# Start, Hyena filters, softmax ends and the last group of a two-block transformer on one core: loads reordered, groups of four, a lag of one chunk

## The chip, the core and the metric

The kernel runs on one core of a Trainium2 chip. Five engines work side by side, each on its own list of instructions: TensorE (PE: matmuls and transposes; its weight loads are shown as PEld), VectorE (DVE), ScalarE (ACT), GpSimd (POOL) and SyncE (SP), which issues most of the transfers (DMA). They wait for each other by semaphores. Data lie in SBUF, matmuls write to PSUM, and inputs, outputs and some intermediate results lie in HBM. The metric is the device time of one execution in microseconds (us), the median of the runs shown.

## What is computed

Two transformer blocks follow one another on x (512 tokens of 1024 channels) with a context of 256 tokens. The first is one layer: retention and mLSTM heads run in both directions after having run over the context, then a SwiGLU feed-forward. The second has four layers with the mixers latent attention (MLA), sliding-window attention (SWA), Hyena, and latent attention again.

```python
# first block, one layer
mod = silu(c) @ w_ada + b_ada                    # six vectors: sh1, sc1, g1, sh2, sc2, g2; the same for ctx
hc = rms_norm(ctx, norm1_gain) * (1 + csc1) + csh1
feats_c = mixer_inputs(hc, w_in, ...)            # keys, values, gates of the context: start states
hx = rms_norm(x, norm1_gain) * (1 + sc1) + sh1
feats_x = mixer_inputs(hx, w_in, ..., rope)      # query, key, value, gate; rope on the retention heads
x = x + g1 * mixer_output(scans(feats_x, states))
x = rms_norm(x + g2 * swiglu(...), final_gain)
# second block
for layer in range(4):
    hx = rmsnorm(x, g_pre[layer]) * (1 + scale_x) + shift_x; hc = ... of ctx
    yx, yc = (mla_mixer, swa_mixer, hyena_mixer, mla_mixer)[layer](hx, hc, ...)
    x = x + gate_x * rmsnorm(yx, g_post[layer])
    ctx = ctx + gate_c * rmsnorm(yc, g_post[layer])      # not in the last layer
# swa: softmax over [context scores, band scores, one sink column]; hyena: two long convolutions with
# filters made by a small sine network from 64 hidden channels, on x and on ctx
```

## The kernel before

Activations lie channel-major: eight tiles of 128 channels by 512 tokens (x) or 256 tokens (context). Almost every matmul is made in three passes of a split operand: a value is cut into a high and a low part (`split`, L396: ACT casts at L397, DVE subtracts at L398), and `mac` (L436) issues high by high, high by low, low by high (L441, L442, L443). Weights come as 512 KB loads into four buffers (`wload`, L400, tile `raw`) and are split into `whi` and `wlo`. Tiles named `b` (128 by 512) have 53 buffers, `t` ten, `P` eight.

The order of the work is written out with generators: `weave` (L192) takes steps of several generators in proportion to the numbers beside them, and `islice` takes only the first steps of one. `self.mods(n)` takes n steps of the stream of modulation vectors (`mod_stream`, L520): each vector takes four steps, each step two loads of 512 KB and 16 matmuls with 32 columns of weights (L504). `need(i)` draws from the stream until vector i is there.

**Start** (`first_block`, L603). SP issues the row vectors (`rows`), the filter network's constants (`filter_setup`, L1776), x, ctx, and then the `w_ada` loads of the first vectors. `load_T` (L476) transposes x and ctx on TensorE, `Rms` (L222) sums squares, and its root is taken by one small matmul (L242), DVE (L244) and POOL (L245), and spread by `over_columns` (L1373). `norm1` (L639) applies norm and modulation to x (L570 and L576 on DVE, L575 on ACT), stores x to HBM (`xd`, L645), and then does the same for the context. `ahead` holds the first key weights. `dense` (L798) makes, for a pair of heads, keys, context keys, values, context values, start states, and then for each head a query and a gate.

**Hyena filters.** `filters` runs beside the feed-forward layer. In `filter_unit` (L1855) each tile takes one matmul with 128 rows of weights (L1873) and one with 64 rows (L1874), which adds the low part.

**Softmax** (`softmax`, L1376) is called once for each head and block of 128 queries: maximum (L1380), its negative times the scale (L1382; with a sink L1384), exponential with its sum (L1385), for a sink one more exponential (L1387) and an add (L1388), and the reciprocal (L1389). `stageA` of MLA and SWA calls it; `stageB` transposes P and multiplies by V. In SWA's `stageB` the low part of P is multiplied by 64 columns of V (L1738, L1741).

**Hyena** (`hyena`, L1907). `conv(i, c)` (L1953) is the two long convolutions of chunk c (256 channels) of x (i = 0, 20 steps) or of the context (i = 1, 14 steps). Chunk c runs beside the projections of chunk c + 1; the last chunk runs beside eight steps of modulation vectors and the preloads of the output projection.

**End** (`layer_end`, L1244). `product(z)` (L1264) multiplies a group of 256 tokens by the output weights, copies to SBUF (L1277) and sums squares; `rest(z)` (L1284) takes the root, scales, adds x from HBM (L1308, L1309) and, in the last layer, `store` (L1333) transposes to token-major (L1340), copies (L1341) and stores (L1342). The `rest` of the last group is left over for the very end.

## Time and profile before

| what | us |
|---|---|
| median of 3 runs | 2915.62 (2914.16 to 2920.24) |
| the profiled execution | 2918.76 |
| its span on the core | 2917.0 |
| TensorE busy | 2787.1 |
| VectorE busy | 1814.9 |
| ScalarE busy | 1334.4 |

The profile is one execution. The kernel is one long list of work for TensorE, in stages that use the other engines to different degrees; TensorE's idle time lies at the two ends and in the attention and Hyena stages. A matmul's shown duration includes the time in which it overlaps its neighbours, so what a matmul costs is read from the distance between the starts of two that follow one another.

### The profile page before, as it was taken

How to read it: one execution, taken by the hardware profiler on the slowest of the kernel's cores; microseconds unless marked ns; L12 is line 12 of the kernel's file. 1: busy time of each engine (PE TensorE's matmuls, PEld its weight loads, DVE VectorE, ACT ScalarE, POOL GpSimd, SP SyncE). 2: the span in 40 equal slices, each digit the busy share in tenths (PEclk: the TensorE clock that was granted, in tenths of full speed). 3: DMA queues.
4: the chain of work that ended last, by engine and by line, in shares of the span. 5: the costliest groups of instructions: out<-in, count | busy, mean ns of one | idle time of the engine just before them, and what ended most of it. 6: DMA issues, size and time to landing. Idle time of an engine off the chain costs nothing. (4 is left out here: it accounts for less than half of the span.)

```text
span 2917.0 us, 44103 instructions
## 1 busy us (share of the span) xinstructions
PE 2787.1 (96%) x17106; PEld 2364.2 (81%) x17106; DVE 1814.9 (62%) x3775; ACT 1334.4 (46%) x2610; POOL 128.8 (4%) x158
## 2 busy tenths in 40 slices
PE   7999999999999999999999999989999998999998
PEld 4888878887777787888889877778888886887887
DVE  6665455555655556246768577788576777754774
ACT  4344344346455433345555566675332223544553
POOL 1000000000000000000000000000021122000000
PEclk8999999999999999999999999999999999999998
DMA  7233232544555536321234241123132226432122
GB/s 264 86 111 123 73 101 84 168 154 141 164 158 163 170 112 209 108 67 44 68 93 156 64 131 42 35 71 117 62 95 84 84 80 195 130 97 63 56 82 69
DMA packets 365830, 318.98 MB, mean 109 GB/s; under 512 B 17511, under 2 KB 326517, under 8 KB 365620
## 3 DMA queue, kind: packets, MB, share of 16 engines
q1 hardware_dynamic: 365204, 315.99, 35.2%
q8 instruction: 134, 2.20, 0.3%
q14 instruction: 76, 0.62, 0.1%
q0 software_dynamic: 416, 0.17, 0.0%
HBM read 273.90 MB, written 42.21 MB: 108 GB/s over the span
## 5 line engine op out<-in xcount | busy, mean ns | idle before, releaser
L441 PE MATMUL mm<-b,whi 128*128 128x512 f32 (+1 forms) x2548 | 895.8, 352 | 4.7 <-ACT whi L397 2.5
L443 PE MATMUL mm<-b,wlo 128*128 128x512 f32 (+1 forms) x2548 | 887.3, 348 | 1.2 <-DVE wlo L398 1.1
L442 PE MATMUL mm<-b,whi 128*128 128x512 f32 (+1 forms) x2548 | 887.6, 348 | 0.0
L441 PEld LDWEIGHTS mm<-b,whi 128*128 128x128 f32 x2548 | 486.1, 191 | 74.4 <-issue 5.8
L443 PEld LDWEIGHTS mm<-b,wlo 128*128 128x128 f32 x2548 | 486.1, 191 | 62.0 <-DVE wlo L398 2.3
L442 PEld LDWEIGHTS mm<-b,whi 128*128 128x128 f32 x2548 | 486.5, 191 | 60.2 <-issue 0.8
L398 DVE TENSOR_TENSOR wlo<-raw,whi 128x1024 fp32r<-128x1024 f32 (+3 forms) x286 | 292.0, 1023 | 239.7 <-ACT whi L397 224.1
L397 ACT CAST whi<-raw 128x1024 fp32r<-128x1024 f32 (+3 forms) x286 | 252.3, 885 | 397.1 <-PE mm L442 253.9
L443 PE MATMUL mm<-b 128*128 128x256 f32 (+1 forms) x628 | 189.4, 302 | 0.5 <-DVE b L398 0.3
L1385 ACT ACTIVATE P<-mm,sm 128x768 f32<-128x768 f32 (+3 forms) x176 | 127.9, 727 | 116.6 <-DVE sm L1382 68.4
L441 PE MATMUL mm<-b 128*128 128x256 f32 (+1 forms) x500 | 158.2, 318 | 8.4 <-ACT P L1385 4.6
L441 PE MATMUL mm<-b,P 128*128 128x256 f32 x560 | 161.8, 289 | 4.0 <-ACT b L575 2.8
L442 PE MATMUL mm<-b,P 128*128 128x256 f32 x560 | 160.4, 286 | 0.9 <-DVE b L576 0.8
L442 PE MATMUL mm<-b 128*128 128x256 f32 (+1 forms) x500 | 153.0, 307 | 0.4 <-DVE b L398 0.3
L1380 DVE TENSOR_REDUCE sm<-mm 128x1 f32<-128x768 f32 (+3 forms) x176 | 128.6, 733 | 39.7 <-PE mm L1583 23.8
L245 POOL TENSOR_TENSOR rs<-rs,mhalf 128x2 f32<-128x2 f32 (+1 forms) x44 | 42.3, 962 | 2427.2 <-DVE rs L244 2279.8
L398 DVE TENSOR_TENSOR t<-mm,t 128x512 fp32r<-128x512 f32 (+1 forms) x208 | 136.5, 663 | 15.3 <-ACT t L397 14.1
L397 ACT CAST t<-mm 128x512 fp32r<-128x512 f32 (+1 forms) x208 | 116.0, 569 | 54.8 <-PE mm L1395 51.6
L235 DVE TENSOR_TENSOR t<-t 128x256 f32<-128x256 f32 (+1 forms) x216 | 92.5, 441 | 71.9 <-ACT t L231 69.4
L1395 PE MATMUL mm<-ct,P 128*128 128x128 f32 x768 | 122.8, 276 | 13.0 <-ACT P L1385 8.2
L231 ACT ACTIVATE t<-b 128x256 f32<-128x256 f32 (+1 forms) x252 | 100.7, 431 | 67.7 <-DVE b L1101 40.9
L443 PEld LDWEIGHTS mm<-b 128*128 128x128 f32 x628 | 120.6, 192 | 5.6 <-DVE b L398 1.3
(351 smaller groups left out, 5129.7 us busy)
## 6 DMA issues: line engine op xcount, KB each, us to landing
raw<-in_w_mod_dram SPq DMA_DIRECT2D x96, 512.0 KB, 4.4
raw<-in_w_ada_dram SPq DMA_DIRECT2D x48, 512.0 KB, 3.9
raw<-in_w_in_dram SPq DMA_DIRECT2D x48, 512.0 KB, 4.0
raw<-in_w_ffn_in_dram SPq DMA_DIRECT2D x44, 512.0 KB, 4.1
raw<-in_c_w_in_dram SPq DMA_DIRECT2D x32, 512.0 KB, 4.3
raw<-in_a_w_in_dram SPq DMA_DIRECT2D x28, 512.0 KB, 4.1
ks<-t SPq DMA_DIRECT2D x48, 256.0 KB, 2.8
raw<-ks SPq DMA_DIRECT2D x24, 512.0 KB, 3.3
```

What stands on the lines that cost most here:

```text
L231: self.k.nc.scalar.activation(sq, x, AF.Square)
L235: self.k.nc.vector.tensor_tensor(self.acc, self.acc, sq, ALU.add)
L245: nc.gpsimd.tensor_tensor(s[:, 4:4 + nt], s[:, :nt], self.k.mhalf[:, :nt], ALU.pow)
L397: self.nc.scalar.copy(dst.hi, src)
L398: self.nc.vector.tensor_tensor(dst.lo, src, dst.hi.bitcast(F32), ALU.subtract)
L441: nc.tensor.matmul(ps, l.hi, r.hi, start=start and i == 0, stop=False)
L442: nc.tensor.matmul(ps, l.hi, r.lo, start=False, stop=False)
L443: nc.tensor.matmul(ps, l.lo, r.hi, start=False, stop=stop and i == n - 1)
L1380: nc.vector.tensor_reduce(s[:, 0:1], S, AX.X, ALU.max)
L1385: nc.scalar.activation(P, S, AF.Exp, bias=s[:, 1:2], scale=scale, accum_out=s[:, 2:3])
L1395: self.nc.tensor.transpose(ps[:, 128 * i:128 * i + 128], b, self.ident)
```

## The change

Five places are edited.

1. **Start.** x is issued first; the row vectors go to ACT's queue, the filter network's constants to POOL's; ctx is issued only behind the first key weights. The context's norm becomes a generator of its own (`norm1c`). The keys of the first pair are multiplied tile by tile as the norm of x gives them, in two PSUM banks; the first query and gate come ahead of the context's keys, beside `norm1c`. The stores of x to HBM come behind that. `mod_stream` gets a stop after the second vector.
2. **Hyena filters.** The low part of the filter weights gets 64 rows of zeros (a memset on POOL), and its matmul takes all 128 rows.
3. **Softmax** ends once for a group of query blocks or heads: one reciprocal of up to four columns; in SWA the four sinks share one add, one exponential and one add. SWA's low-part matmul takes all 128 columns of V.
4. **Hyena.** The context's convolution of a chunk runs a chunk later; three modulation steps move into the chunk loops, five stay at the end.
5. **End.** The last group of the last layer goes through `last`: each product is scaled by the gate on DVE and squared on ACT straight from PSUM, transposed (`turn`) to token-major in two PSUM tiles, and x is transposed beside it; behind the root four operations of 512 columns scale, add x and are stored on two queues.

```diff
@@ mod_stream
             self.have.add(i)
+            if i == 1:
+                yield
@@ first_block
-        first = self.rows(False, nc.sync)
+        inputs = [self.load_T(I["x"][0], N, X), self.load_T(I["ctx"][0], NC, C)]
+        next(inputs[0])
+        first = self.rows(False, nc.scalar)
         next(first)
-        setup = self.filter_setup()
+        self.second_setup()
+        setup = self.filter_setup(nc.gpsimd)
         next(setup)
...
-        weave((chain(inputs[0], sums(rms[0], X)), 17), (islice(units, U0), U0), self.mods(MA))
+        weave((chain(inputs[0], sums(rms[0], X)), 17), self.mods(M0 - 3))
         self.log_sigmoid(lg, lgt, 8)
-        mods = chain(self.mods(M0 - MA)[0], root(rms[0]), self.mods(8 - M0)[0])
-        weave((chain(inputs[1], sums(rms[1], C)), 17), (islice(units, U1), UW * U1), (mods, 9 - MA))
-        rms[1].root()
+        mods = chain(self.mods(3)[0], root(rms[0]), self.mods(8 - M0)[0])
+        weave((islice(units, U0), U0), (mods, 12 - M0))
         W = I["w_in"][0]
         ahead = [self.wv(W, 512)]
-        weave((norm1(), 16), (islice(units, UB), UB))
+        next(inputs[1])
@@ dense
+            if out == {(pair, ml): o}:
+                banks = [self.mm() for _ in range(2)]
+                for k, _ in enumerate(norm1()):
+                    for u in range(2):
+                        self.mac(banks[u], [(wk[k][:, 128 * u:128 * u + 128], hx[k])], k == 0, k == KT - 1)
+                    yield
...
+            if banks:
+                yield from query(0)
             kc = kv_ctx(wk)
@@ first_block
-        weave((dense(0, False), ND), (chain(idle(GD), gates()), 10 + GD), (units, UC))
+        start = dense(0, False)
+        weave((islice(start, KT), KT))
+        cf.update(tables())
+        weave((islice(start, 4), 4), (norm1c(), 28), (units, 2))
+        for k in range(KT):
+            nc.sync.dma_start(self.xd[k], X[k])
+        X.clear()
+        weave((start, ND - 4), (chain(idle(GD), gates()), 10 + GD), (units, UC))
@@ filter_head, filter_unit
-            ws.append((w, l[0:64, :]))
+            nc.gpsimd.memset(l[64:128, :].bitcast(F32), 0.0)
+            ws.append((w, l))
-                        nc.tensor.matmul(ps, x[0:64, :], l, start=False, stop=True)
+                        nc.tensor.matmul(ps, x, l, start=False, stop=True)
@@ softmax (step for each block, end for the group)
+        def step(j, S, P):
+            b = top[:, 4 + j:5 + j]
+            nc.vector.tensor_reduce(top[:, j:j + 1], S, AX.X, ALU.max)
...
+            nc.scalar.activation(P, S, AF.Exp, bias=b, scale=scale, accum_out=sums[:, j:j + 1])
+        def end(rd):
+            if sink is not None:
+                nc.vector.tensor_tensor(top[:, 0:n], sink, top[:, 4:4 + n], ALU.add)
+                nc.scalar.activation(top[:, 0:n], top[:, 0:n], AF.Exp)
+                nc.vector.tensor_tensor(sums[:, 0:n], sums[:, 0:n], top[:, 0:n], ALU.add)
+            nc.vector.reciprocal(rd[:, 0:n], sums[:, 0:n])
@@ swa stageB
+                    nc.tensor.matmul(out, v[:, g], p.hi, start=z == LS, stop=False)
+                    nc.tensor.matmul(out, v[:, g], p.lo, start=False, stop=z == nb + LS - 1)
@@ hyena
-            cv = mix((conv(0, c), 20), (conv(1, c), 14))
-            weave((cv, HC), (dense(c + 1), 16))
+            cv = mix((conv(0, c), 20), (conv(1, c - 1), 14) if c else (None, 1))
+            weave((cv, HC), (dense(c + 1), 16), (islice(bg[0], c), c) if c else (None, 1))
         cv = conv(0, 3)
-        weave((conv(1, 3), 14), (islice(cv, HT), HT), bg, (end, 3 + 3 * AP))
-        return cv, 20 - HT
+        weave((chain(conv(1, 2), conv(1, 3)), 28), (islice(cv, HT + 3), HT + 3), (islice(bg[0], 5), 5), (end, 3 + 3 * AP))
+        return cv, 17 - HT
@@ last (new; called in place of the last product and its rest)
+        for k in range(KT):
+            ps = proj(k)
+            y = self.t(256)
+            nc.vector.tensor_scalar(y, ps, G[:, k:k + 1], None, ALU.mult)
+            rs.add(ps)
+            ys.append((k, y))
+            if len(ys) > 1:
+                turn(*ys.pop(0))
+            if k < 4:
...
+            yield
+        turn(*ys.pop(0))
+        rs.root()
+        for h in range(2):
+            for j in range(2):
+                o = xt[j, h]
+                nc.vector.scalar_tensor_tensor(o, T[j][:, 512 * h:512 * h + 512], rs.cols[j], o, ALU.mult, ALU.add)
+                (nc.scalar if j else nc.sync).dma_start(self.out[t0 + 128 * j:t0 + 128 * j + 128, 512 * h:512 * h + 512], o)
```

## Rows read from the trace of the kernel before

**Rows 1.** The page: busy time of each engine, share of the span, instructions.

```profile
PE 2787.1 (96%) x17106; PEld 2364.2 (81%) x17106; DVE 1814.9 (62%) x3775; ACT 1334.4 (46%) x2610; POOL 128.8 (4%) x158
```

**Rows 2.** Busy time by stage: stretch, its length; each engine's busy time; clock, DMA.

```profile
653.00:1005.00 352.00, 352.00 (x1606) 264.60 (x1606) 197.69 (x291) 188.14 (x253) 0.00 (x0) 1.00 0.51 160
1295.00:1505.00 210.00, 201.95 (x1244) 174.25 (x1243) 143.25 (x321) 116.09 (x252) 0.00 (x0) 0.99 0.21 64
1640.00:1995.00 355.00, 323.41 (x2066) 271.48 (x2065) 268.32 (x729) 220.78 (x547) 0.80 (x1) 0.98 0.24 72
2108.00:2207.00 99.00, 98.56 (x607) 87.85 (x607) 70.95 (x126) 30.38 (x51) 21.01 (x24) 1.00 0.30 92
2411.00:2455.00 44.00, 33.90 (x237) 21.59 (x236) 31.59 (x70) 10.90 (x22) 12.59 (x16) 0.88 0.76 245
```

**Rows 3.** Timeline of SP's queue at the start: start, length, line, transfer, count.

```profile
8.24 3.75 SPq L484 DMA_DIRECT2D b<-in_x_dram  x8
...
15.74 26.07 SPq L403 DMA_DIRECT2D raw<-in_w_ada_dram  x16
...
47.12 2.30 SPq L403 DMA_DIRECT2D raw<-in_w_ada_dram  x2
```

**Rows 4.** Timeline at the start; in brackets the engine's idle time before, and its cause.

```profile
27.69 1.93 PE L504 MATMUL mm<-raw,condc 128*32 128x256 f32 x16 [2.93 <-ACT t L1801]
...
51.79 1.08 PE L504 MATMUL mm<-raw,condc 128*32 128x256 f32 x8 [1.53 <-DMA raw<-in_w_ada_dram]
...
53.95 0.75 DVE L570 SCALAR_TENSOR_TENSOR t<-b,G,mm 128x512 f32<-128x512 f32 x1 [0.95 <-PE mm L1373]
...
56.73 0.77 PE L441 MATMUL mm<-b,whi 128*128 128x512 f32 x1
...
69.97 0.28 PE L441 MATMUL mm<-whi,b 128*128 128x256 f32 x1
```

**Rows 5.** Timeline of TensorE around one filter pair.

```profile
666.78 0.39 PE L443 MATMUL mm<-b,wlo 128*128 128x512 f32 x1
667.01 0.40 PE L1873 MATMUL mm<-b 128*128 128x512 f32 x1
667.34 0.50 PE L1874 MATMUL mm<-b 64*128 64x512 f32 x1
667.77 0.50 PE L441 MATMUL mm<-P,b 128*128 128x512 f32 x1
668.10 0.39 PE L442 MATMUL mm<-P,b 128*128 128x512 f32 x1
```

**Rows 6.** Waits, 1640 to 1995 us: who for whom, total us, times, longest.

```profile
PE mm L1713 <- ACT P L1385: 9.5, 11, 1.6
PE mm L1741 <- DVE t L398: 7.9, 10, 2.0
...
DVE sm L1388 <- ACT sm L1387: 16.5, 22, 1.4
```

**Rows 7.** Groups by line and shape, 1640 to 1995 us: count, busy us, mean ns.

```profile
L1387 ACT ACTIVATE sm<-sink,sm 128x1 f32<-128x1 f32 x96 | 27.6, 288 | 1.1 <-DVE sm L1384 1.0
...
L1389 DVE RECIPROCAL rd<-sm 128x1 f32<-128x1 f32 x96 | 14.9, 157 | 1.2
```

**Rows 8.** Groups by line and shape, DVE, a Hyena chunk (2108 to 2207 us).

```profile
L398 DVE TENSOR_TENSOR wlo<-raw,whi 128x1024 fp32r<-128x1024 f32 x9 | 11.5, 1279 | 4.5 <-ACT whi L397 4.5
L1993 DVE TENSOR_TENSOR t<-mm,raw 128x512 f32<-128x512 f32 x12 | 8.2, 681 | 0.6 <-PE mm L443 0.6
```

**Rows 9.** Timeline of the end.

```profile
2885.61 0.82 PE L1340 MATMUL mm<-ct,b 128*128 128x128 f32 x6
...
2902.40 0.61 PE L242 MATMUL mm<-mean,t 128*128 128x1 f32 x4 [1.37 <-DVE t L235]
...
2904.57 0.87 DVE L1308 SCALAR_TENSOR_TENSOR b<-b,mod,mm 128x256 f32<-128x256 f32 x2 [1.30 <-PE mm L1373]
...
2909.05 4.70 SPq L1342 DMA_DIRECT2D out_dram<-b  x4
```

More of the change, by code (lines that the diff above doesn't have):

```diff
@@ L647, in norm1 @@
-            X.clear()
+            yield from self.apply(X, rms[0].rstd(), N, G1[:, 0, :], mv[0][:, 0, :], hx, KT)
+        todo = [(0, 0), (0, 1), (1, 0), (1, 1)]
+        units = chain(setup, self.filters(todo[:FS], 1), late)
+        weave((chain(inputs[0], sums(rms[0], X)), 17), self.mods(M0 - 3))
+        self.log_sigmoid(lg, lgt, 8)
+        mods = chain(self.mods(3)[0], root(rms[0]), self.mods(8 - M0)[0])
+        weave((islice(units, U0), U0), (mods, 12 - M0))
+        W = I["w_in"][0]
@@ L648, in norm1, with norm1c @@
+        ahead = [self.wv(W, 512)]
+        next(inputs[1])
+        def norm1c():
+            yield from inputs[1]
+            yield from sums(rms[1], C)
+            yield
+            rms[1].root()
+            yield
+            yield
+            G1 = have["G1"]
             yield from self.apply(C, rms[1].rstd(), NC, G1[:, 1, :], mv[0][:, 1, :], hc, KT)
             C.clear()
-        todo = [(0, 0), (0, 1), (1, 0), (1, 1)]
-        units = chain(setup, self.filters(todo[:FS], 1), late)
@@ L653, in first_block @@
[L653 to L665 removed]
+        have = {}
@@ L668, in first_block, with tables @@
+        cf = {}
+        def tables():
+            for k, (o, n) in self.coff["first"].items():
+                if n == 512:
+                    t = self.b()
+                    nc.sync.dma_start(t, I["k_first"][:, o:o + n])
+                    yield k, t
         RH = self.bhl()
@@ L850, in dense @@
                 yield
[L851 to L876 removed]
+            for u in range(1 if banks else 0, 2):
+                yield from query(u)
         out = {}
@@ L1269, in product @@
             act = [x[:, s] for x in acts.pop(z) + [self.kept.pop((i, t0))] for s in (slice(0, 256), slice(256, 512))]
+            o.rs = Rms(self, 256, D)
+            if l == 3 and z == len(groups) - 1:
+                yield from self.last(lambda k: self.proj(ws[k], act, 256), t0, o.rs, m[2][:, 0, :])
+                return
             o.y = [self.b() for _ in range(KT // 2)]
-            o.rs = Rms(self, 256, D)
             for k in (5, 6, 7, 3, 4, 0, 1, 2) if z == len(groups) - 1 else (0, 1, 2, 5, 6, 7, 3, 4) if z else range(KT):
@@ L1574, in stageA @@
             o["P", i], o["rd", i] = [], self.sp.tile([128, 4], F32, tag="rd", name="rd")
+            step, end = self.softmax(n // 128, scale)
             for qt in range(n // 128):
@@ L1585, in stageA @@
                 P = self.P(tot)
-                self.softmax(ps[:, off:off + tot], P, o["rd", i][:, qt:qt + 1], scale)
+                step(qt, ps[:, off:off + tot], P)
                 o["P", i].append(P)
+                if qt == n // 128 - 1:
+                    end(o["rd", i])
                 yield
@@ L1708, in stageA @@
             rd = self.sp.tile([128, 4], F32, tag="rd", name="rd")
+            step, end = self.softmax(4, scale, self.sink[:, 4 * g:4 * g + 4], nsink[:, 4 * g:4 * g + 4])
             for v in range(4):
@@ L1720, in stageA @@
                 P = self.P(nb + 256)
-                h = 4 * g + v
-                self.softmax(ps[:, 512 - nb:768], P, rd[:, v:v + 1], scale, (self.sink[:, h:h + 1], nsink[:, h:h + 1]))
+                step(v, ps[:, 512 - nb:768], P)
                 Ps.append(P)
+                if v == 3:
+                    end(rd)
                 yield
```

134 lines of the change are left out of this document (66 added, 68 removed).

## The prediction

> **What bounds the kernel now.** I read the page first: TensorE (PE) is busy 2787 of 2917 us, VectorE (DVE) 1815, ScalarE (ACT) 1334 [rows 1]. An edit off TensorE's path is worth nothing, except where TensorE waits or is slowed, so I looked for those places next, with the busy time by stage [rows 2]. The stage that builds the Hyena filters beside the feed-forward layer (653 to 1005 us) has TensorE busy the whole time: only work taken off TensorE counts there. The sliding-window attention (1640 to 1995) has 323.4 of 355 us busy, so 31.6 us of waiting; latent attention (1295 to 1505) 8 us; a Hyena chunk (2108 to 2207) 0.4 us; the end of Hyena (2411 to 2455) 10.1 us. Then the two ends: before 56.73 us TensorE has only small work [rows 4], and after its last projection the kernel needs another 16 us [rows 9].
>
> **The profiled execution** took 2918.76 us, 2917.0 of it the span. The sum is made against 2918.8; the median of the runs, 2915.6, is 3.1 lower, and I take those 3 us off at the end.
>
> **1. Start of the kernel: -11 us (-4 to -17).** In the queue of SP, x is issued at 8.24 us, behind row vectors and filter constants, and `w_ada` at 15.74, behind x and ctx [rows 3]. The 16 loads of 512 KB (8.4 MB) then last 26.07 us, so some 320 GB/s: this stream is what the scale vector of the norm, and with it the first key, waits for. In the changed kernel x stands right behind the first constants (about 1.2 us), so 7.0 us are gone; with ctx moved behind the key weights, 15.74 - 8.24 - 3.75 = 3.7 us more. The row vectors move to ACT's queue and the filter constants to POOL's; behind them wait the first transposes and the filter's sine, of which the load stream needs neither. Second, `need(1)` now returns before the third vector's first step: today its matmuls (L504 at 51.79) wait 1.53 us for a load and stand ahead of the broadcast of the root (L1373, then L570 at 53.95) [rows 4]; that is 2.5 us. Third, the filter's sine steps leave the middle of the load stream, where a step of it waited 2.9 us for them [rows 4] and its buffers could not be filled again. Sum 16; against it 1.5 us, since the split of the key weights (two operations of 1.28 us on DVE, [rows 8]) will now fall among the norm's steps. So the first key matmul comes some 15 us earlier, near 42 us. Interleaving keys with the norm by itself I cost at nothing: today they already begin as the norm proceeds (56.73 to 69.97, [rows 4]).
>
> What is given back: TensorE work that lay in idle time now lies in the full stream. It is 16 transposes of ctx (1.9 us at 0.12), two small filter matmul pairs, late row transposes, ctx's means and 16 matmuls of the third vector, about 4 us together. Late next is DVE: it has to do ropes, two weight splits, ctx's sums and ctx's norm while TensorE has only one query and one gate; that could keep the whole gain down to 4. The eight stores of x are put behind the gate's weights and ahead of the value weights in SP's queue; the context's key product and, where ready, later projections cover them. Uncovered they would cost up to 6 us, which is the low end.
>
> **2. Filter matmuls with all 128 rows: -19 us (-17 to -20).** A pair L1873/L1874 is a full matmul and one whose weights have 64 rows. The full one ahead of the pair takes 0.23 us from start to start; from there on the distances are 0.33, 0.43 and 0.33 [rows 5]. Each of the three is longer than 0.23, together by 0.40 us; 48 pairs make 19.2 us, in a stage where TensorE never waits. With zeros in the other 64 rows the matmul still has 512 columns, so 0.23. The eight memsets go to POOL, which does nothing in that stage [rows 2], six steps ahead of their use. In SWA the matmul with 64 columns, L1741, becomes a full one as well: what the rows show there is waiting for its operand (7.9 us, [rows 6]), which stays, so I count its form at 0.
>
> The Trainium skill speaks both ways. TensorEngine Tiling (Array Packing), Key Properties, says that a change of tiling mode drains TensorE, which the three long distances agree with. But TensorE: Matmul & The Clock Gate, Part 3, has it that a matmul with few rows takes as long as one with 128, and advises packing, not padding; by that alone this part would bring 0. That is a rival below.
>
> **3. Softmax ends in groups of four: SWA -13 us (0 to -26), latent attention -3 (0 to -8).** In SWA each of 96 softmaxes ends with an ACT exponential of one column (0.288 us), an add on DVE and a reciprocal (0.157 us, L1389) [rows 7]; DVE stands 16.5 us waiting for that exponential [rows 6]. In groups of four, three quarters of the exponentials (20.7 us of ACT), three quarters of the reciprocals (11.2 us) and of the wait (12.4), and half the adds (7 us, if one lasts as long as a reciprocal) go: some 31 us of DVE's in-order time. Work off DVE is worth what TensorE waits for DVE and ACT: P 9.5 us at L1713 and `t` 7.9 at L1741 [rows 6], and the rest of the 31.6 us [rows 2] is mostly of these kinds. At most 26 us of it; at least 0, if the maximum and the exponential themselves are the chain. I take half, as the queue ahead of both shrinks but their own durations stay. Latent attention loses 56 reciprocals (8.7 us of DVE), but TensorE waits only 8 us there; I take 3 for its two layers.
>
> **4. Context's convolutions a chunk later: +1 us (-5 to +9).** TensorE's work is only moved. A context convolution is 12 matmuls of 512 columns at 0.23 and 40 small ones at 0.12, some 7 us of TensorE. Loop 0 gives one up (-7); loops 1 and 2 exchange like for like and take three steps of the modulation (+3.3 at 1.1); the stage behind gives up three of the last convolution's twenty steps (about -3.6). So 7.3 us go around the end, and the end takes 14.3 less 3.3 more work. Today it waits 10.1 of its 44 us [rows 2]; if half of that is filled, the change gains 5. But DVE is busy 31.6 of the 44 us [rows 2], and a context convolution brings some 15 us of DVE: 8 of the 24 products L1993/L1994 (12 each) at 0.68 us [rows 8], 5.4 us, and about 10 in its sums and splits (an estimate from these). With the three steps (about 4 us) that is 51 us of DVE, so I let the end grow by 8, against 7.3 saved around it. The two context convolutions also follow one another there, and the output projection's first group waits for the second; that is the +9.
>
> **5. Token-major end: -3 us (-1 to -6).** Today the last matmul ends at 2902.40 - 1.37 = 2901.0; the scaled rows start at 2904.57, and the last of four stores is issued by 2913.75 [rows 9]. In between lie eight pairs of DVE operations, sixteen transposes and four copies. After: the root comes about 0.4 us earlier (no copy ahead of the square), then four DVE operations of 512 columns at some 0.8 us (two of 256 take 0.87 [rows 9]), so the last store near 2907.4, 6.3 us earlier. But 16 transposes of x and 14 of y move into the full loop ahead: 30 at 0.12 (six in 0.82 with the last one's tail, [rows 9]), 3.6 us. The wait for the x loads lies under the projections.
>
> Sum: -11 - 19 - 13 - 3 + 1 - 3 = -48; 2918.8 - 48 = 2870.8, less 3.1: **2868 us**.
>
> **Rivals.**
> - **SWA's waits stay** (part 3 gives 0): the maximum, L1380 and the exponential, are the chain, and another wait ends where these ended. For it: DVE and ACT wait for each other there in many places. 2868 + 16 = 2884.
> - **The start is DVE's**: TensorE starts early and then waits for the norm and ropes, part 1 gives 4. 2875. Against it: it is the same DVE work as today, begun earlier, and TensorE has a query and a gate more beside it.
> - **A 64-row matmul is no dearer** (the rule above), the long distances come from the accumulation, and part 2 gives 0: 2887. Against it: the full matmul accumulates too, and the one after the pair does not belong to it.
> - **The end on the other side: buffers in Hyena.** The lag keeps three more 512-column buffers alive in loops 1 and 2; I count 30 for activations and tables, 18 for two chunks, 4 in the convolution, so 52 of 53 today and 55 then. If the next chunk's projections (about 68 us of TensorE in a loop of 99) have to wait for the convolutions instead of running beside them (34 steps take about 65 us alone, by the 23 in 44 us at the end), a loop lasts up to 133 us, +34, twice: +68, and 2936. It makes the kernel slower once the projections stand still for over seven tenths of that. Against it: buffers come free as the convolution advances, and the peak of 55 would be short.
>
> **How the numbers follow.** Chances: forecast 0.60, SWA's waits stay 0.16, the start is DVE's 0.13, the 64-row rule 0.04, buffers 0.05 (0.03 of it beyond the old time), and 0.02 that the gains cancel otherwise. A measurement of this kernel can tell about 0.2% (6 us) from no change. All but the last two are faster: 0.94, same 0.02, slower 0.04. Range: the wide terms are SWA (13 each way), the end of Hyena (8) and the start (7), together some 17 us, and the upper side takes in the second to fourth cases: 2845 to 2892.
>
> **What would show it.** Right: `w_ada` issued near 5 us and first key matmul near 42; L1873 to L1874 at 0.23; L1387 and L1389 down to 24 in SWA and the stage at about 340 us; Hyena's loop 0 at 92 us and its end at over 50; from the last projection to the end 10 us instead of 16. Wrong: DVE full and TensorE idle between 50 and 75 us; the filter stage as long as before; SWA still with 30 us of waiting; loops 1 and 2 of Hyena longer than 103 us.

## The result and the profile after

The changed kernel takes 2954.39 us (median of 4 runs, 2951.12 to 2964.32) against 2917.29 for the kernel before beside it; the ratio is 1.0135, with a 95% interval of 1.0112 to 1.0159. By the medians it is 37 us slower, by the ratio **39 us**; the prediction was 2868 us, 48 faster. Gains and losses below go by the ratios, each against runs of the kernel before beside it. One run of `e6_start_ctx` (3112.27 us at a granted clock of 0.839, where its other three have 0.979 to 0.982) fell in a slower state and is left out of its figures. The profiled execution has a span of 2952.9 us, 35.9 more than before.

The page, busy time of each engine, to be held against [rows 1]:

```profile
PE 2785.2 (94%) x17120; PEld 2375.6 (80%) x17120; DVE 1792.9 (61%) x3593; ACT 1319.7 (45%) x2531; POOL 136.0 (5%) x174
```

TensorE, VectorE and ScalarE are each busy a little less than before. So the 36 us are time in which TensorE waits, and they have to be looked for by stage. Busy time by stage of the changed kernel, columns as in [rows 2]: the filter stage, sliding-window attention, Hyena's loop 0, its loop 2 and its end.

```profile
682.00:1024.00 342.00, 340.48 (x1624) 268.94 (x1623) 198.58 (x290) 188.85 (x255) 3.12 (x6) 1.00 0.53 166
1649.00:2004.00 355.00, 324.12 (x2082) 275.41 (x2081) 261.88 (x617) 210.21 (x481) 0.70 (x1) 0.99 0.24 72
2124.00:2225.00 101.00, 95.11 (x541) 82.42 (x540) 57.94 (x93) 26.18 (x43) 13.30 (x16) 0.97 0.25 78
2325.00:2426.00 101.00, 100.93 (x630) 88.19 (x628) 67.53 (x124) 27.48 (x46) 20.19 (x24) 1.00 0.31 97
2426.00:2498.00 72.00, 53.15 (x316) 38.30 (x314) 48.33 (x112) 14.01 (x28) 18.22 (x24) 0.83 0.46 146
```

Loop 0 has 66 matmuls fewer than a chunk before (541 against 607 in [rows 2]) and is no shorter; the end has grown from 44 to 72 us.

How much each stage gained or lost is read by taking the same instruction of both programs and subtracting its start in the one trace from that in the other. The difference is -6 us at the first key matmul, +25 from 145 to 590 us, +29 where the filter stage begins, +14 behind it, +9 behind sliding-window attention, +39 behind Hyena, and +36 behind the last layer's attention and at the end. Two single traces also drift against each other where nothing was edited: `e11_end`, whose only edit is at the very end, stands 2.7 us behind the kernel before at 300 us, 4.8 at 700 and 0.8 at 2800. So a stage's difference of 4 us or less says little. The last column is what each part does by itself, from experiments below (ratio less 1, times 2918 us):

| part | predicted | in the changed kernel, by the two traces | alone, by the ratio |
|---|---|---|---|
| 1. start | -11 | +25 | +25 (`e1_start`) |
| 2. filter matmuls | -19 | -14 | -14 (`e3_filt`) |
| 3. softmax ends | -16 | -4 in sliding-window attention | -3 (`e4_soft`) |
| 4. Hyena's lag | +1 | +30 | +31 (`e2_lag`) |
| 5. end | -3 | 0 | -1 (`e11_end`) |
| sum | -48 | +37, with small differences between stages +36 | +38 |

The last layer's latent attention is 2.8 us shorter in the changed kernel, but 2.4 in `e1_start` and 3.4 in `e3_filt`, which have the old softmax, so part 3 gets nothing for it.

The parts add up: +38 alone, +39 together. The intervals of the five ratios make some 11 us together, so an interaction below that would not be seen. Two parts cost what I had not seen in them, and a third brings little.

### The profile page after: what moved, and what is told of

Same layout as the page of the kernel before. It is cut to its first block, busy times and chain, and to the rows that moved or that the text cites. A ratio compares the mean times of both kernels' runs of the same rounds, so it can differ in the third digit from the quotient of the medians.

```text
span 2952.9 us, 43839 instructions
## 1 busy us (share of the span) xinstructions
PE 2785.2 (94%) x17120; PEld 2375.6 (80%) x17120; DVE 1792.9 (61%) x3593; ACT 1319.7 (45%) x2531; POOL 136.0 (5%) x174
## 5 line engine op out<-in xcount | busy, mean ns | idle before, releaser
L398 DVE TENSOR_TENSOR wlo<-raw,whi 128x1024 fp32r<-128x1024 f32 (+3 forms) x286 | 292.1, 1024 | 264.5 <-ACT whi L397 248.7
L441 PE MATMUL mm<-b 128*128 128x256 f32 (+1 forms) x500 | 159.6, 322 | 10.6 <-ACT b L397 6.3
```

Of the source, the lines that this page charges most:

```text
L398: self.nc.vector.tensor_tensor(dst.lo, src, dst.hi.bitcast(F32), ALU.subtract)
L441: nc.tensor.matmul(ps, l.hi, r.hi, start=start and i == 0, stop=False)
```

## The experiments

### Each part alone

Each of these four kernels is the kernel before with one part of the diff shown above, nothing else.

> The kernel before with the start of the change alone (loads of x first, vectors on the queues of ACT and POOL, first keys, query and gate ahead of the context's norm, stores of x behind them). Theory: the loss of some 25 us that the trace of the changed kernel shows up to 145 us belongs to this part by itself, so the time is 2940 to 2946 and the same three long waits of TensorE stand in the trace: for the context's sums of squares (L242, about 5 us), and twice for the gates' chain (about 4 and 6 us). Rival (my prediction's own working): the start brings 4 to 17 us, and the loss in the changed kernel comes from what the other parts do to it (the filter constants, buffers): then 2901 to 2913.

Measured: 2945.44 us, ratio 1.0085 (1.0068 to 1.0101). The loss is the start's own, and the three long waits are in its trace (4.7, 4.3 and 4.6 us). The rival falls.

> The kernel before with Hyena's lag alone (the context's convolution a chunk later, steps of the modulation in loops 1 and 2, the last two context convolutions one after the other at the end). Theory: Hyena loses about 30 us by this part alone, 2945 to 2950: loop 0 stays at 100 us although it has one convolution less, the end grows from 42 to about 71 us. Rival (the prediction's working): the end grows by 8, loop 0 gives 7 back, so 2912 to 2927, and the rest of the loss comes from the other parts.

Measured: 2951.59 us, ratio 1.0108 (1.0084 to 1.0132). Loop 0 lasts 100.7 us (100.2 before), the end 70.6 (42.4 before). The rival falls.

> The kernel before with the filter matmuls over all 128 rows alone. Theory: the pair L1873/L1874 gives back what the trace of the changed kernel shows, 14 us, so 2901 to 2905. The prediction's working: 19 us, 2896 to 2901. Rival (a matmul with 64 rows costs no more than one with 128): 2917.

Measured: 2902.11 us, ratio 0.9953 (0.9932 to 0.9974), so 13.7 us faster. In its trace the stage is 14 us shorter. The rival falls: between these matmuls one with 64 rows costs more than one with 128. My 19 was too high.

> The kernel before with the softmaxes' ends in groups of four alone, in both kinds of attention, and the full matmul in place of the one with 64 columns. Theory: DVE's wait for the small exponential goes and ACT's wait for the maximum and the bias grows in its place, so TensorE waits as long for P as before; 4 to 7 us in all, 2910 to 2914. The prediction's working: 16 us, 2901. Rival: the full matmul costs what the groups gain, 2917.

Measured: 2917.24 us, ratio 0.9991 (0.9981 to 1.0001), so 0 to 5 us. That is nearer to the rival's number than to the theory's, but the full matmul isn't what eats the gain: from the last matmul in front of it to L1741 the median distance is 0.314 us before and in the changed kernel. What does is looked for in the waits, below.

### What the start waits for

Two edits of `e1_start`, then both, then the query and gate put back.

```
-        weave((start, ND - 4), (chain(idle(GD), gates()), 10 + GD), (units, UC))
-        weave((dense(1, False), ND), (ret_chain(0), NR), self.mods(4))
+        weave((start, ND - 4), (units, UC))
+        weave((dense(1, False), ND), (ret_chain(0), NR), (chain(idle(GD), gates()), 10 + GD), self.mods(4))
```

> The kernel before with the changed start (as e1_start) and one edit: the chain of the mLSTM gates goes beside the second pair of retention heads and not beside what the early query and gate left of the first. Theory (the gates' chain of small DVE and ACT steps, some 35 us long, has lost the query and the gate that covered it): the waits at L719 (4.3 us) and L761 (4.6) and the low clock behind each go, 12 to 16 us off e1_start's 2945, so 2929 to 2933. Rival (DVE is short of time at the start, so the same DVE work only delays something else): within 4 us of 2945.

Measured: 2940.41 us, ratio 1.0070 (1.0053 to 1.0087), 4 us better than `e1_start` by the ratios; 6 to 7 by the traces (from +22.5 to +15.9 at 200 us and +16.7 at 300). The two longest of TensorE's waits from 50 to 260 us in this kernel:

```profile
PE mm L242 <- DVE t L235: 4.7, 1, 4.7
PE mm L761 <- ACT t L758: 2.8, 1, 2.8
```

The waits between 120 and 160 us are gone, but 2.8 us of the gates' chain stand at the new place, at 210 us, with matmuls at low clock behind (0.63 of full from 215 to 218). A third to a half of what the theory said; the rival isn't wholly wrong.

```
         next(inputs[0])
+        next(inputs[1])
...
-        weave((islice(units, U0), U0), (mods, 12 - M0))
+        weave((chain(inputs[1], sums(rms[1], C)), 17), (islice(units, U0), U0), (mods, 12 - M0))
+        rms[1].root()
```

> The kernel before with the changed start (as e1_start) and one edit: the context is loaded right behind x, and its sums of squares and their root are put where they were in the kernel before, ahead of x's norm; the context's norm itself stays behind the first query and gate. Theory (these sums stand behind the ropes on DVE, TensorE waits 2.0 and 4.7 us for them and then runs at the low clock): 8 to 11 us off, less 3 to 4 for the later `w_ada`, so 2936 to 2942. Rival (the context's norm is late by DVE's whole queue, so the next wait takes the place of this one): within 3 us of 2945.

Measured: 2939.42 us, ratio 1.0074 (1.0051 to 1.0097); 3 us better by the ratios, 9 by the traces (from +22.5 to +13.7). Of TensorE's waits, 40 to 160 us:

```profile
PE mm L441 <- DVE t L787: 4.8, 2, 4.2
...
PE mm L441 <- ACT b L577: 3.7, 1, 3.7
```

In place of the 4.7 us at L242 there are 3.0 at the same line further ahead, and new ones have come: the first key now waits 3.7 us for the norm of x (in `e1_start` 2.6) and comes at 54.05 us (48.65), and a key matmul waits 4.2 for a rope. The waits for the gates' chain stay. Partly the rival's picture: DVE takes the steps in one order or in another, and something waits for the last of them.

> The kernel before with the changed start and both edits, of e5_start_gates (gates' chain beside the second pair) and of e6_start_ctx (context loaded right behind x, its sums ahead of x's norm). If the two repairs work on different waits, their gains of 6.6 and 8.7 us by the traces add up: 2925 to 2932. If each only moves the wait on to the next step, as DVE's queue would: 2938 or more.

Measured: 2932.89 us, ratio 1.0054 (1.0034 to 1.0075); by the traces +11.8 in place of +22.5. The gains of the two edits add up in part (10.7 of 15.3 us). With both repairs the start is still 12 to 16 us behind the kernel before. Over the distances of TensorE's instructions from the first key to 230 us, 12 us more than before lie above what full clock and no gap would give: 4 at the wait for the rope, and 8 to 9 between 180 and 220 us, at the gates' new place (12.2, where the same work before has 3.6).

```
-            if banks:
-                yield from query(0)
...
-        weave((islice(start, 4), 4), (norm1c(), 28), (units, 2))
+        weave((islice(start, 2), 2), (norm1c(), 28), (units, 2))
```

> The kernel before with the changed start (as e1_start), but the first query and gate stay behind the context's keys and values, where they were in the kernel before. Theory (the query and gate were the cover of the gates' chain; ahead of the context's norm something has to stand in their place): the waits at L719 and L761 shrink by most of their 9 us, but TensorE waits some 11 us longer for the context's norm, so 2940 to 2950. Rival (taking them forward is the whole loss): 2915 to 2925.

Measured: 2946.04 us, ratio 1.0104 (1.0084 to 1.0125). Mostly as the theory has it: the wait at L761 falls from 4.6 to 0.3 us, the one at L719 only from 4.3 to 3.8, and idle time moves forward, to the context's norm. Busy time of TensorE (second number) and DVE (fourth) of this kernel, 70 to 90 us:

```profile
70.00:80.00 10.00, 3.47 (x12) 2.00 (x12) 8.62 (x22) 6.72 (x18) 0.00 (x0) 0.61 0.00 1
80.00:90.00 10.00, 2.60 (x10) 2.09 (x11) 8.61 (x24) 5.06 (x11) 0.73 (x1) 0.50 0.07 7
```

So taking the query and the gate forward isn't the loss by itself: put back, they cover the second half of the gates' chain, but then nothing stands beside the context's norm. One query and one gate (some 11 us of TensorE) don't cover both. In the kernel before, the norm of the context followed that of x at once, and the keys of x covered it.

The loads alone (x and context first in SP's queue, vectors in ACT's and POOL's, the order of the work as before):

```
+        inputs = [self.load_T(I["x"][0], N, X), self.load_T(I["ctx"][0], NC, C)]
+        for g in inputs:
+            next(g)
-        first = self.rows(False, nc.sync)
+        first = self.rows(False, nc.scalar)
...
-        setup = self.filter_setup()
+        setup = self.filter_setup(nc.gpsimd)
```

> The kernel before with the loads of the changed start alone: x and the context first in SP's queue, the row vectors in ACT's, the filter constants in POOL's, and the third vector of the modulation no longer ahead of the norm; the order of keys, context, query and gate stays as before. Theory (the loads are worth the few us by which the first key comes earlier, 4 to 6, and the loss at the start is all in the order of the work behind it): 2911 to 2916. Rival (loads issued from three queues delay one another and the row vectors that TensorE's first transposes need): 2918 to 2922.

Measured: 2924.56 us, ratio 1.0021 (1.0010 to 1.0033), 6 us slower. SP's queue of this kernel:

```profile
1.18 8.69 SPq L484 DMA_DIRECT2D b<-in_x_dram  x8
...
15.56 6.82 SPq L647 DMA_DIRECT2D xd<-b  x7
...
32.55 13.72 SPq L403 DMA_DIRECT2D raw<-in_w_ada_dram  x10
```

It isn't a clean test: with x there early, the eight stores of x, which need only x, slid forward into the stream of `w_ada`, where they take some 7 us of the queue, and the first key comes 3.5 us later than before. What the loads would be worth without that is open.

### What Hyena waits for

```
-            weave((cv, HC), (dense(c + 1), 16), (islice(bg[0], c), c) if c else (None, 1))
+            weave((cv, HC if c else 20), (dense(c + 1), 16), (islice(bg[0], c), c) if c else (None, 1))
```

> The kernel before with Hyena's lag (as e2_lag) and one number changed: in loop 0 the convolution's steps are laid out by a weight of 20, its own count, not 38. Theory (the weight of 38 was for both convolutions; with one left, its 20 steps come in the first half of the loop, too dense for its own chain through DVE, POOL and ACT, and TensorE waits): loop 0 falls from 100 us to 93 or 94, so 2944 to 2946. Rival (the waits belong to the tables or to the convolution's first use of the filter constants): loop 0 stays at 100, 2951.

Measured: 2940.25 us, ratio 1.0066 (1.0046 to 1.0085), 12 us better than `e2_lag`. Loop 0 takes 87.3 us; TensorE is busy all of it:

```profile
2113.00:2200.00 87.00, 87.00 (x517) 77.39 (x516) 54.97 (x87) 26.20 (x41) 11.84 (x16) 1.00 0.28 82
```

```
-            cv = mix((conv(0, c), 20), (conv(1, c - 1), 14) if c else (None, 1))
+            cv = mix((conv(0, c), 20), (conv(1, 0), 14) if c == 1 else (chain(conv(1, 1), conv(1, 2)), 28) if c else (None, 1))
...
-        weave((chain(conv(1, 2), conv(1, 3)), 28), (islice(cv, HT + 3), HT + 3), ...
+        weave((conv(1, 3), 14), (islice(cv, HT + 3), HT + 3), ...
```

> The kernel before with Hyena's lag (as e2_lag) and one edit: the context's third convolution runs in loop 2 behind the second, beside the last chunk's projections, so the end has one context convolution as in the kernel before. Theory (at the end the two context convolutions are one chain of dependent small steps with nothing to cover it): the end falls from 71 to about 45 us, loop 2 grows by the 7 us of TensorE that a context convolution has, so 2930 to 2934. Rival (DVE is the bound, the work costs its DVE time wherever it stands): loop 2 grows by 15 us or more and the sum stays above 2940.

Measured: 2949.26 us, ratio 1.0100 (1.0084 to 1.0116), not what either side said. The loops table below shows why: loop 2 did not grow (98.4 us) and the end stayed at 75. The convolution was in loop 2 by its place in the code, but by the loop's weight (38 for now 48 steps) its last ten steps still came behind the projections. So it doesn't decide between the two sides.

`e9_lag_fix` has this edit, the weight of 20 in loop 0, and 53 in loop 2.

> The kernel before with Hyena's lag and both repairs: loop 0's convolution laid out by its own count of 20 steps, and the context's third convolution in loop 2 with the weight of that loop raised from 38 to 53, so that its steps really lie beside the last chunk's projections (in e8_lag_end, by the trace, ten of them still came after these). Theory (the loss is the chain of small dependent steps with nothing beside it): loop 0 at 87 to 93 us, loop 2 at 106 to 110, the end back to 42 to 46; Hyena as long as before or up to 6 us shorter, so 2910 to 2921. Rival (a chunk's delay itself costs, through buffers or DVE): still 2935 or more.

Measured: 2930.00 us, ratio 1.0041 (1.0026 to 1.0057): 20 us better than `e2_lag`, and 12 slower than the kernel before; neither side's number.

`e15_lag_mods` is `e9_lag_fix` with the modulation's steps and three steps of the last convolution left where they were:

```
-            weave((cv, (20, HC, 53)[c]), (dense(c + 1), 16), (islice(bg[0], c), c) if c else (None, 1))
+            weave((cv, (20, HC, 53)[c]), (dense(c + 1), 16))
...
-        weave((conv(1, 3), 14), (islice(cv, HT + 3), HT + 3), (islice(bg[0], 5), 5), (end, 3 + 3 * AP))
-        return cv, 17 - HT
+        weave((conv(1, 3), 14), (islice(cv, HT), HT), bg, (end, 3 + 3 * AP))
+        return cv, 20 - HT
```

> The kernel before with the context's convolutions moved as in e9_lag_fix (none in loop 0, the first in loop 1, the second and third in loop 2), but the modulation's steps and nine steps of the last convolution stay in the end as they were. Theory (the modulation's matmuls are what TensorE did at the end while the convolutions' chain was waiting; in the loops they only cost their time): 4 to 8 us off e9_lag_fix's 2930, so 2918 to 2926, no slower than the kernel before by more than what a delay costs in loops 0 to 2. Rival (the delay of a chunk itself costs): 2930 or more.

Measured: 2919.35 us, ratio 1.0004 (0.9995 to 1.0014). Laid out so, the delay of a chunk costs nothing that can be measured; it brings nothing either. Length in us of the loops (from the last evacuation of a chunk's projections to that of the next), of the end (from there to the last context transform) and of what follows to the last sum of the last convolution:

| kernel | loop 0 | loop 1 | loop 2 | end | behind | sum |
|---|---|---|---|---|---|---|
| before | 100.2 | 99.0 | 98.2 | 42.4 | 46.4 | 386 |
| changed | 101.1 | 100.5 | 101.1 | 71.5 | 41.8 | 416 |
| `e2_lag` | 100.7 | 100.3 | 101.2 | 70.6 | 42.1 | 415 |
| `e7_lag_weight` | 87.3 | 103.2 | 101.2 | 71.3 | 42.8 | 406 |
| `e8_lag_end` | 101.3 | 100.4 | 98.4 | 75.2 | 43.4 | 419 |
| `e9_lag_fix` | 87.3 | 103.0 | 113.1 | 51.0 | 42.4 | 397 |
| `e15_lag_mods` | 88.5 | 101.9 | 108.3 | 43.1 | 45.9 | 388 |

From `e9_lag_fix` to `e15_lag_mods` loop 1 gets 1.1 us shorter, loop 2 4.8 and the end 7.9, while what is behind grows by 3.5. The edit moves two things, three steps of the modulation from the loops to the end and three steps of the last convolution out of the end, so how much of the end's 7.9 us is due to which isn't shown. The third context convolution beside loop 2's projections costs that loop 10 us; in the end, beside nothing, it was worth 20 (71.3 against 51.0). The two context convolutions side by side at the end, in place of one after the other, were not tried.

### The end, and a version that beats both

> The kernel before with the token-major end alone. Theory, from the trace of the changed kernel: the last product takes 6.4 us more, the way from it to the end 6.5 less, so no change, 2916 to 2920. The prediction's working: 3 us faster, 2914 to 2917. Rival (the products of the last group wait for the transposes' banks): 2922.

Measured: 2916.41 us, ratio 0.9995 (0.9986 to 1.0004). No change that can be measured.

The changed kernel without its start and without the lag (parts 2, 3 and 5):

> The changed kernel without its start and without Hyena's lag: the filter matmuls, the softmaxes and the end remain. Theory (the parts add): the filters' 14 to 16 us, the softmaxes' 1 to 4 and nothing from the end, so 2898 to 2903, a ratio of 0.993 to 0.995, faster than both kernels. The prediction's working for these parts: 38 us, 2880. Rival (the gain of the filters is eaten by a later wait once the other parts stand beside it): 2910 or more.

Measured: 2898.21 us, ratio 0.9928 (0.9916 to 0.9940): **21 us faster than the kernel before and 60 faster than the changed one** by the ratios (20 and 56 by the medians). The three parts alone make 17.8; nothing of the filters' gain is eaten.

## Why the prediction was wrong

**Part 1, the start (-11 predicted, +25).** Three steps failed. The first is the price of x's issue. SP's queue in the changed kernel, to be held against [rows 3]:

```profile
1.17 8.13 SPq L484 DMA_DIRECT2D b<-in_x_dram  x8
9.35 27.31 SPq L403 DMA_DIRECT2D raw<-in_w_ada_dram  x16
...
47.28 8.38 SPq L1067 DMA_DIRECT2D xd<-b  x8
```

I moved x's loads with the 3.75 us that they took behind the small ones. In the first place they take 8.13, so `w_ada` starts at 9.35, not near 5, and its stream lasts 1.2 us longer. The Trainium skill (DMA: Bandwidth & Descriptors, Issuing engines are not separate DMA queues) says that spreading loads over several engines' queues saves no more than the time of issuing them; the trace agrees: of the 10.7 us of issues that I took from ahead of `w_ada`, 6.4 were saved. The second is the sine. I had said that its steps leave the middle of the load stream, for 2.9 us. Its matmuls still stand among those of `w_ada`, and its five steps on DVE (44.08 to 46.84 us) now stand ahead of the last partial sum of the second vector (L509), for which TensorE waits:

```profile
26.95 1.96 PE L1899 MATMUL mm<-t,fw 33*64 33x512 f32 x2
38.91 1.97 PE L1903 MATMUL mm<-t,fw 64*64 64x512 f32 x2
46.76 0.40 DVE L509 TENSOR_TENSOR acc<-acc,mm 128x256 f32<-128x256 f32 x1
47.22 0.69 PE L513 MATMUL mm<-ct,acc 128*128 128x128 f32 x2 [1.83 <-DVE acc L509]
```

From the last issue of `w_ada` to this L513 10.6 us pass, where the kernel before needs 7.8 (L513 at 49.57). The third vector's 2.5 us did come: from L513 to the first key it is 3.5 us, before 7.2. Together with the stream's -6.4 and +1.2 that makes -6: the first key comes at 50.72 us and not near 42, 6 us earlier and not 15. The third step is the one that decides: "what is given back" held only TensorE's work, and put the lateness of DVE, which it names, at 7 us of the gain at most. Timeline of TensorE in the changed kernel from the first key on:

```profile
50.72 1.22 PE L441 MATMUL mm<-b,whi 128*128 128x512 f32 x2 [1.96 <-ACT b L577]
...
84.41 0.98 PE L242 MATMUL mm<-mean,t 128*128 128x1 f32 x4 [4.73 <-DVE t L235]
...
87.96 0.63 PE L443 MATMUL mm<-b,wlo 128*128 128x512 f32 x1
88.39 0.63 PE L441 MATMUL mm<-b,whi 128*128 128x512 f32 x1
...
136.08 1.46 PE L719 MATMUL mm<-ct,P 128*64 128x128 f32 x6 [4.34 <-DVE P L709]
...
151.22 0.69 PE L761 MATMUL mm<-ct,t 64*128 64x64 f32 x4 [5.64 <-ACT t L758]
```

The context's sums of squares now stand behind x's ropes on DVE, and TensorE waits 4.73 us for them. The gates' chain, which runs from 118 to 152 us through DVE and ACT in small steps, has lost the query and the gate beside it, and TensorE waits 4.34 and 5.64 us. Busy time in two stretches of it, before (TensorE full) and after:

```profile
130.00:140.00 10.00, 10.00 (x60) 7.35 (x58) 1.91 (x3) 2.60 (x5) 0.00 (x0) 1.00 0.17 53
140.00:150.00 10.00, 10.00 (x61) 8.96 (x62) 5.73 (x14) 3.71 (x8) 0.00 (x0) 1.00 0.50 159
```

```profile
130.00:140.00 10.00, 5.66 (x34) 4.95 (x32) 7.66 (x29) 4.21 (x10) 0.00 (x0) 0.83 0.35 107
140.00:150.00 10.00, 5.58 (x25) 4.25 (x24) 9.87 (x18) 2.47 (x5) 0.00 (x0) 0.96 0.00 0
```

The long waits cost a second time: behind the one at L242 the matmuls of 512 columns (87.96, 88.39) stand 0.43 us apart in place of 0.23, until 91 us. Added up over the distances of TensorE's instructions from 50 to 165 us, 35 us lie over what full clock and no gap would give (some 19 of it in six waits of 1 us and more), against 7 from the first key to 150 us before. 28 more, less the 6 us gained at the first key, leave 22; the other 3 are near my estimate of 4 for the work moved in. The Trainium skill (TensorE: Matmul & The Clock Gate, Part 1) gives 0.427 and 0.216 us for these distances at the two clock levels; the trace's 0.43 agrees, and its 0.23 is a little more.

The rival "the start is DVE's" named the place, but it still gave 4 us of gain. Nor has DVE more to do: from 50 to 150 us DVE is busy 64 of 100 us in `e1_start` and 70 in the kernel before. It isn't the amount of DVE's work, it is which of its steps TensorE has nothing beside. The stores of x (8.38 us of the queue) did no harm: TensorE waits for no transfer between 50 and 160 us. `e5_start_gates`, `e6_start_ctx` and `e13_start_both` show it for some 10 of the 25 us, by giving them back. For the 12 to 16 us that stay with both repairs it is read from the trace alone (the rope's wait and the gates' new place, above); no run gives these back.

**Part 2, the filters (-19 predicted, -14).** The mechanism was right. TensorE in the changed kernel around one pair, as [rows 5]:

```profile
694.45 0.39 PE L1961 MATMUL mm<-b 128*128 128x512 f32 x1
694.68 0.40 PE L1962 MATMUL mm<-b 128*128 128x512 f32 x1
694.91 0.39 PE L441 MATMUL mm<-P,b 128*128 128x512 f32 x1
695.15 0.39 PE L442 MATMUL mm<-P,b 128*128 128x512 f32 x1
```

The distances are 0.23 or 0.24, as forecast, here and around 36 of the 48 pairs. The term was mis-sized: the excess around the pairs adds up to 20 us in the trace of before, as my sum has it, but after the change some 8 us of the same stage still lie over the full-clock distance, where the kernel before has 23 in all: 3 around the pairs, and 2 more than before elsewhere. I had set that remainder to nothing. Some 2 us of it come of waits that I had ruled out by "a stage where TensorE never waits": with the pairs faster, TensorE now waits for casts of ACT, from 682 to 1024 us:

```profile
PE mm L441 <- ACT P L397: 1.0, 4, 0.4
```

Another 0.9 us stands at eight pairs that follow matmuls with 32 columns of weights (L504): from L1961 to the next matmul it is 0.34 us there. The Trainium skill's rule that few rows take as long as many (TensorE: Matmul & The Clock Gate, Why this matters for your kernels, where it is said of 32 rows; my text named Part 3) gives 0 for this part; `e3_filt` measured 13.7 us, so here, between full matmuls, the measurement decides against it.

**Part 3, the softmaxes (-16 predicted, -3, with an interval from -5 to 0).** The rival "SWA's waits stay" came true, and with it the sign of being wrong that I had named, 30 us of waiting: 355 less 324.12 are 30.9 us, before 31.6. The groups are what was forecast, 24 in place of the 96 of [rows 7]:

```profile
L1471 ACT ACTIVATE sm<-sm 128x4 f32<-128x4 f32 x24 | 4.8, 200 | 0.6 <-DVE sm L1470 0.4
L1473 DVE RECIPROCAL rd<-sums 128x4 f32<-128x4 f32 x24 | 4.1, 171 | 0.3
```

But the waits, to be held against [rows 6] and against this row of before:

```profile
ACT P L1385 <- DVE sm L1384: 39.3, 35, 3.2
```

```profile
ACT P L1466 <- DVE sm L1465: 51.5, 58, 2.5
...
PE mm L1802 <- ACT P L1466: 10.2, 15, 1.3
...
PE mm L1828 <- DVE t L398: 6.0, 10, 1.8
...
DVE sums L1472 <- ACT sm L1471: 5.3, 5, 1.6
```

DVE's wait for the small exponential falls from 16.5 to 5.3 us. ACT's wait for the maximum and bias, 39.3 us before, is 51.5 (50.7 in `e4_soft`): what DVE and ACT are freed of at one end of the softmax, ACT waits for at the other. TensorE's wait for P stays (9.5, now 10.2). Its wait for `t` gives 1.9 us at the matmul with the low part (L1741, now L1828), but at the one with the high part (L1739, now L1827) it grows from 3.5 to 6.0, so that all waits for `t` make 11.8 us before and 12.0 after. I had taken the middle of 0 and 26 without a row that spoke for the middle; the row on ACT's 39.3 us stood in the same view and named the end of the chain that stays.

**Part 4, Hyena (+1 predicted, +30).** My sum: loop 0 -7, loops +3.3, behind -3.6, end +8. Measured: loop 0 +0.9, loops 1 and 2 +4.4, behind -4.6, end +29.1. Loops and rear were near; two terms failed. (The "14.3 less 3.3" of TensorE's work in the end is wrong by my own terms, 7 and 3.6 less 3.3 are 7.3; it did not enter the sum.)

Loop 0: I took a convolution's TensorE time off, but its weight of 38 in the loop's layout stayed for 20 steps, so that these came 1.7 times as dense as before (34 steps by the same weight); TensorE waits for the convolution's own chain (POOL, then ACT's split) in a chunk that had waited 0.4 us [rows 2]. Its only wait in loop 0:

```profile
PE mm L441 <- ACT P L397: 5.8, 3, 2.7
```

`e7_lag_weight` changes nothing else and loop 0 falls to 87.3.

The end: I counted DVE, and counted it well: 51 us forecast, 48.33 in the row above. But I took its idle time for room. DVE was busy 31.6 of 44 us [rows 2], 72%, and it is 67% busy in the longer end; TensorE 77% and 74%. The end is a chain of small steps that hand over to one another, and its length went with the work in it: 44 x 48.33 / 31.59 = 67 us would have been the better estimate. The same scaling gives 51 us for the end of `e9_lag_fix`, which takes 51:

```profile
2417.00:2468.00 51.00, 37.88 (x239) 28.23 (x232) 36.80 (x77) 12.19 (x23) 12.98 (x16) 0.87 0.52 160
```

TensorE's busy time would give 69 and 49 us, so the rows don't tell by which engine to scale; and it is an estimate that fits, not a cause that was tested: another order of the steps in the end was not tried. The longest of its waits are short and of every kind:

```profile
PE mm L2102 <- DVE t L2082: 3.4, 2, 2.2
PE mm L2102 <- POOL P L2084: 2.9, 3, 1.6
PE mm L504 <- DMA raw<-in_w_mod_dram: 2.8, 4, 1.3
```

and the granted clock is 0.83 of full in it, 0.88 before. And the modulation's matmuls, which I costed at 3.3 us in the loops, cost 5.9 there (loops 1 and 2 from `e9_lag_fix` to `e15_lag_mods`), while in the end, where TensorE waits, they cost nothing that shows. `e15_lag_mods` puts them back, and with the third convolution beside loop 2 the end is as it was:

```profile
2304.00:2412.00 108.00, 105.75 (x645) 93.55 (x643) 79.99 (x156) 28.23 (x52) 25.21 (x32) 1.00 0.27 82
2412.00:2456.00 44.00, 33.83 (x231) 21.48 (x231) 31.05 (x69) 10.41 (x20) 12.58 (x16) 0.88 0.77 248
```

The rival on the other side, buffers, fell: loops 1 and 2 last 100.5 and 101.1 us, 4.4 more than before, and the modulation's three steps alone cost up to 5.9. I had given a slower kernel 0.04, 0.03 of it for this mechanism, which doesn't show. (The chances of the four faster cases add to 0.93, where I wrote 0.94.)

**Part 5, the end (-3 predicted, 0).** The way from the last product to the end is as forecast. Timeline of the end, to be held against [rows 9]:

```profile
2944.96 0.61 PE L242 MATMUL mm<-mean,t 128*128 128x1 f32 x4 [0.50 <-DVE t L235]
...
2946.65 2.73 DVE L1406 SCALAR_TENSOR_TENSOR b<-mm,rs,b 128x512 f32<-128x512 f32 x4 [0.81 <-POOL rs L245]
2947.43 1.65 SPq L1407 DMA_DIRECT2D out_dram<-b  x2
2948.09 1.69 ACTq L1407 DMA_DIRECT2D out_dram<-b  x2
```

The root's sums, four operations of DVE and four stores on two queues are all that is left; the last store is issued 6.6 us behind the start of the last product's last matmul (2949.8 against 2943.2), where it took 13 before: 6.4 earlier, as forecast. But the full loop ahead grew by 6.5 us, where I had 30 transposes at 0.12, 3.6. The transposes are as forecast: 28 of them in the loop, 0.11 us each, 3.2. What I had not counted is the root of the group before. Its sums of squares (L242) stood behind the first 24 matmuls of the last group; the first step of `last` has loads and no matmul, so TensorE waits for them, and then runs at low clock. Before, then after, then the granted clock (the last but two) after:

```profile
2876.84 0.50 PE L242 MATMUL mm<-mean,t 128*128 128x1 f32 x4
```

```profile
2911.44 0.61 PE L242 MATMUL mm<-mean,t 128*128 128x1 f32 x4 [1.37 <-DVE t L235]
```

```profile
2915.00:2920.00 5.00, 4.86 (x32) 4.43 (x31) 3.86 (x11) 0.87 (x2) 0.00 (x0) 0.75 0.00 0
```

The wait takes 1.5 us from start to start over a full-clock distance, and from 2914.2 to 2917.4 us matmuls of 256 columns stand 0.21 us apart in place of 0.12, 1.5 us in all. By this sum the part would bring the 3 us that I forecast without these two; no run tests it.

## What to carry to other kernels

In a stage that is one chain of small steps, the idle time of the engines was not room. When work was put in, the stage kept about its busy share (44 us with DVE 72% busy became 72 us at 67%, and 51 at 72% in `e9_lag_fix`); so scale such a stage by its work, as a first estimate, and don't fill it. Before a step is moved, name what TensorE has beside it at its new place, and what it covered at the old one. The context's norm, moved behind the keys, was left with one query and one gate (11 us), and these were then missing beside the gates' chain; by the trace, a first step of `last` without a matmul cost some 3 us. And when a stage loses steps, the weights by which its steps are laid out have to be set anew: that number alone was 12 us here.

## What was not expected of the hardware

- The issue of eight loads of 256 KB takes 3.75 us behind the small loads [rows 3], and 8.13 or 8.69 us (`e10_start_loads`) in the first place of SP's queue, while ACT's and POOL's queues issue small ones. Whether the place or the other queues do it was not tested.
- The first transposes of TensorE, which wait for the row vectors, start at 11.18 us in the changed kernel (5.95 before), so the first tiles of x, issued 7 us earlier, are transposed no earlier (11.38 against 11.24).
- Behind TensorE's wait of 4.73 us the granted clock is 0.55 from 84 to 88 us and 0.60 from 88 to 92, so close to the lower of its two levels (1.2 of 2.4 GHz), and 0.50 from 152 to 156 behind the wait of 5.64: such a wait is dearer than its length.
